# FFN entry in a two-layer decoder step: the chunk made beside the last tokens' sub-layer, in ordinary form

## Chip, cores and metric

The kernel runs on one NeuronCore of a Trainium2 chip. The metric is the time of one execution on the device in microseconds (us). Five engines work side by side, each on its own queue: TensorE (PE; its weight loads are PEld), VectorE (DVE), ScalarE (ACT), GpSimd (POOL) and SyncE (SP), which here issues most of the transfers. TensorE runs at one of two clock levels, 1.2 and 2.4 GHz; a granted clock of 1.00 is the upper one, 0.50 the lower.

## What is computed

One inference step over 1024 prompt tokens and 32 sample tokens, 1056 in all, model width 1024. Layer 0 mixes by pooling and a state-space recurrence, layer 1 by dilated attention; each ends in a SwiGLU feed-forward part (FFN) with 2816 hidden units. What matters here is the end of each mixing sub-layer and the start of its FFN:

```python
hp = hp + rms_norm(y_p, g[1])
hp = hp + rms_norm(swiglu_ffn(rms_norm(hp, g[2]), w_gate, w_up, w_down), g[3])
def swiglu_ffn(x, w_gate, w_up, w_down):
    return (jax.nn.silu(x @ w_gate) * (x @ w_up)) @ w_down
```

## The kernel before

**Numbers in two halves.** Every fp32 operand of a matmul is held as a rounded part `hi` and a rest `lo`, and a product is three matmuls (`mm3`, lines 171 to 173): hi by hi, lo by hi, hi by lo. A weight block is split by a cast on ACT (line 1140) and a subtraction on POOL or DVE (line 1141).

**Tokens.** The tokens are cut into four quarters: 0 and 2 of 256 columns, 1 and 3 of 272 (256 prompt tokens and 16 of the sample). Quarters 0 and 2 form pair 0, quarters 1 and 3 pair 1. Tile i is 128 tokens of a quarter; tile 8 is the 32 sample tokens.

**Seven products.** The FFN's first part multiplies a chunk of 256 hidden units (11 chunks, c = 0 to 10) by all tokens, once for the gate and once for up. It uses a scheme with seven products of 2 by 2 blocks in place of eight. Class `Blocks` keeps the blocks of the activations: B11 and B21 (the two halves of the features of the pair's first quarter), B22 (of the second) and the sums T1 to T4. Class `Weights` makes the sums S1 to S4 of the weights (four DVE additions, lines 1147, 1148, 1153, 1154, and the splits). `seven` runs the products; each is 12 matmuls for one pair, evacuated from PSUM by an addition on DVE (line 1172) or a copy on ACT (line 1174). `hidden` runs the gate and the up products of a chunk, applies silu (line 1195), multiplies the two (line 1199) and stores the result by a transfer from ACT's queue (line 1201).

**The boundary of a tile** (class `Boundary`, put in a pipeline by `Tiles`): `turn` transposes the projected tile on PE (line 318); `stats` takes its mean square (lines 207 to 211); `scale` and `residual` (lines 327 and 331) norm it and add the stream h; `stats2` and `scale2` (line 342) norm it for the FFN; `turn2` transposes it back (line 349); `first` splits it into blocks (lines 265 to 275), `second` (lines 279 to 281) and `third` (lines 286, 287) make T1 to T4 and split them. The transposes of all tiles share two PSUM buffers, `xs` and `tmp` have one buffer each, `h` two.

**The order.** `proj_out` projects quarters 0 and 2, then 1, then 3, each followed by the boundary of its tiles. Before the boundary of quarter 3 it yields to `ffn`, which first issues chunks 0 and 1 for pair 0, gate and up, in the projection's PSUM banks; then come the boundaries of tiles 6, 8 and 7, the last tokens. After them the PSUM banks are changed, and the FFN goes on with chunk 1 for pair 1 (its gate loaded a second time), chunk 0 for pair 1 (both weights loaded a second time), and chunks 2 to 10 for both pairs at once. The instructions are written in this order; a planner that simulates the engines then sets the order on each queue, by what its model finds ready.

Of the kernel before, what the change touches and what calls it, by code (L numbers as in the profile page):

```python
# [9 lines left out]
F32 = mybir.dt.float32  # L10
BF16 = mybir.dt.bfloat16
F32R = mybir.dt.float32r
AF = mybir.ActivationFunctionType
# [11 lines left out]
P = 128  # L25
# [12 lines left out]
HALF = NT // 2  # L38
HID = 2816
HT = HID // P  # L40
# [14 lines left out]
def dram_ap(base, offset, pattern):  # L55
    return bass.AP(tensor=base.tensor, offset=base.offset + offset, ap=[list(x) for x in pattern])
# [3 lines left out]
def step_kernel(ctx, tc, x_prompt, x_sample, state_pool, state_s5, cache_k, cache_v, norm_gains,  # L60
# [4 lines left out]
    nc = tc.nc  # L65
    taps = taps or {}
    V, A, G, T = nc.vector, nc.scalar, nc.gpsimd, nc.tensor
    mult, add, sub = ALU.mult, ALU.add, ALU.subtract
# [10 lines left out]
    wpool = ctx.enter_context(tc.tile_pool(name="wpool", bufs=3))  # L79
# [17 lines left out]
    def nm(s):  # L97
        uid[0] += 1
        return f"{s}_{uid[0]}"

    def mmbank():
        return banks[-1].pool.tile([P, 512], F32, name=nm("mm"), tag="mm", bufs=banks[-1].mm)
# [67 lines left out]
    def mm3(ps, wh, wl, xh, xl, start, stop):  # L170
        T.matmul(ps, wh, xh, start=start, stop=False)  # L171
        T.matmul(ps, wl, xh, start=False, stop=False)  # L172
        T.matmul(ps, wh, xl, start=False, stop=stop)  # L173
# [66 lines left out]
    class Blocks:  # L240
# [1 line left out]


        def __init__(self, xp, Y):
            self.xp, self.blk, self.made = xp, {}, {}
            self.homes = {0: (((Y.pool, "q0"), ("B11", "B21")), ((Y.pool, "q2"), ("T1", "T2")),
                              ((xp, "xc"), ("B22", "T3")), ((xp, "xd"), ("T4",))),
                          1: (((Y.pool, "q1"), ("B11", "B21")), ((Y.pool, "q3"), ("T1", "T2")),
                              ((xp, "xa"), ("T3",)), ((xp, "xb"), ("B22",)), ((xp, "xe"), ("T4",)))}
# [11 lines left out]
        def left(self, pair, c, pt):  # L261
            self.get("B11", pair)
            t = self.made[pair, ("B11", "B21")]
            hi, lo, src = t[:, :, 0, :, c], t[:, :, 1, :, c], pt.rearrange("p (a k) c -> p a k c", a=2)
            A.copy(hi, src)
            V.tensor_tensor(lo, src, hi.bitcast(F32), op=sub)

        def right1(self, part, pt, tmp):
            bc, t3, b11, b21 = tmp
# [19 lines left out]
        def first(self, i, pt, state):  # L289
            pair = 1 if i == 8 else i // 2 % 2  # L290
            c = slice(256, 272) if i == 8 else slice(i % 2 * P, i % 2 * P + P)
            if i < 4 or i == 8:
                self.left(pair, c, pt[:, :, 0:16] if i == 8 else pt)
            if i >= 4:
                state["part"] = lambda n, e: self.get(n, pair)[e][:, :, c]
                t = self.xp.tile([P, 4, 4, c.stop - c.start], F32, name=nm("tmp"), tag="tmp", bufs=1)
                state["tmp"] = [t[:, v] for v in range(4)]
                self.right1(state["part"], pt[:, :, 16:32] if i == 8 else pt, state["tmp"])

        def second(self, i, state):  # L300
            if state:
# [164 lines left out]
    for src in (lambda_re, lambda_im):  # L466
        raw = ptile("lamraw", P)
# [153 lines left out]
    for v, dst in enumerate((c1, c2)):  # L621
        pt = mmbank()
# [16 lines left out]
    for j in range(2):  # L639
# [6 lines left out]
        pt = mmbank()  # L646
# [470 lines left out]
    def ffn(layer, xS, Y, poc, after, side):  # L1117
# [6 lines left out]
        class Weights:  # L1124
# [6 lines left out]
            def split(self, early=False):  # L1131
                r0, r1 = (four(r) for r in self.raws)
                a11, a21, a12, a22 = r0[:, :, 0], r0[:, :, 1], r1[:, :, 0], r1[:, :, 1]
                new = lambda n: wpool.tile([P, 1024], F32R, name=nm(n), tag=n, bufs=4)

                def pair(src, two=True):
                    hi, lo = (new(n).rearrange("p (k i c) -> p k i c", k=4, i=2) for n in ("whi", "wlo"))
                    if not two:
                        hi, lo = hi[:, :, 0], lo[:, :, 0]
                    A.copy(hi, src)  # L1140
                    (V if early and src is S34 else G).tensor_tensor(lo, src, hi.bitcast(F32), op=sub)  # L1141
                    return hi, lo

                half = lambda t, i: (t[0][:, :, i], t[1][:, :, i])
                S12, S34 = (xS.pool.tile([P, 4, 2, P], F32, name=nm(n), tag=n, bufs=1) for n in ("S12", "S34"))
                self.w = {"A11": pair(a11, False)}
                V.tensor_tensor(S12[:, :, 0], a21, a22, op=add)
                V.tensor_tensor(S12[:, :, 1], S12[:, :, 0], a11, op=sub)
                t = pair(S12)
                self.w["S1"], self.w["S2"] = half(t, 0), half(t, 1)  # L1150
                t = pair(r1)
                self.w["A12"], self.w["A22"] = half(t, 0), half(t, 1)
                V.tensor_tensor(S34[:, :, 0], a11, a21, op=sub)
                V.tensor_tensor(S34[:, :, 1], a12, S12[:, :, 1], op=sub)
                t = pair(S34)
                self.w["S3"], self.w["S4"] = half(t, 0), half(t, 1)

        def seven(w, pairs, bank, C, evac):

            def prod(a, b):  # L1160
                ps = bank()
                o = 0
                for pair in pairs:
                    wh, wl = w.w[a]
                    bh, bl = blk[b, pair]
                    n = QUARTERS[pair][1]
                    for k in range(4):
                        mm3(ps[:, o:o + n], wh[:, k], wl[:, k], bh[:, k], bl[:, k], k == 0, k == 3)
                    o += n
                return ps  # L1170

            plus = lambda o, ps, x: V.tensor_tensor(o, ps, x, op=add)  # L1172
            c11, c22, c12, c21 = C
            A.copy(c11, prod("A11", "B11"))
            plus(c22, prod("S2", "T2"), c11)
            plus(c11, prod("A12", "B21"), c11)
            evac(c11, 0, 0)
            plus(c21, prod("S3", "T3"), c22)
            p5 = prod("S1", "T1")
            plus(c12, p5, c22)  # L1180
            plus(c22, p5, c21)
            evac(c22, 1, 1)
            plus(c12, prod("S4", "B22"), c12)
            evac(c12, 0, 1)
            plus(c21, prod("A22", "T4"), c21)
            evac(c21, 1, 0)

        def hidden(c, first, second, pairs, bank, tiles):

            t1, t2 = tiles(), tiles()  # L1190
            got = dict(zip(((0, 0), (1, 1), (0, 1), (1, 0)), t1))

            def act(w, o):
                if w.gate:
                    A.activation(o, o, AF.Silu)

            def put(o, i, j):
                act(second, o)
                (V if i == j == 0 or c < 2 else G).tensor_tensor(o, o, got[i, j], op=mult)
                o0 = j * HALF + (256 if pairs[0] else 0)  # L1200
                nc.scalar.dma_start(hd[2 * c + i][:, o0:o0 + o.shape[-1]], o)

            together = first.gate and pairs == (0,)
            seven(first, pairs, bank, t1, lambda o, i, j: None if together else act(first, o))
            if together:
                act(first, ct[:, 0:4])
            seven(second, pairs, bank, t2, put)

        def raws(kind):
            if kind:  # L1210
                t = xS.pool.tile([P, 2, 4, 256], F32, name=nm("raw2"), tag=kind, bufs=1)
                return [t[:, h] for h in range(2)]
            return [wraw().rearrange("p (k c) -> p k c", k=4) for _ in range(2)]
# [3 lines left out]
            x.split(c < 2 if w is w_gate else c == 1)  # L1217
            return x

        single = lambda: mmbank()[:, 0:256]  # L1220
        parts = lambda: iter([[ct[:, j] for j in range(4 * e, 4 * e + 4)] for e in range(2)]).__next__
        for c in range(2):
            wg, wu = split(w_gate, c, None), split(w_up, c, None if c else "xe")
            hidden(c, wg, wu, (0,), single, parts())
        for _ in poc:
            pass
        po.close()
# [2 lines left out]
        gb = Banks(nm("psumg"))  # L1230
        big = lambda: [f.pool.tile([P, HALF], F32, name=nm("c"), tag=f"c{j}", bufs=2) for j in range(4)]
        two = lambda: gb.pool.tile([P, 1024], F32, name=nm("pp"), tag="pp", bufs=4)[:, 256:256 + HALF]
        for c in (1, 0):
            if c == 0:
                wu = split(w_up, c, "tmp")
            hidden(c, wu, split(w_gate, c, None), (1,), lambda: two()[:, 256:HALF], lambda: [t[:, 256:HALF] for t in big()])
        for c in range(2, HT // 2):
            hidden(c, split(w_gate, c, None), split(w_up, c, "tmp"), (0, 1), two, big)
        gb.close()
        f.close()  # L1240
# [627 lines left out]
    class Chunk:  # L1868
# [12 lines left out]
        def parts(self):  # L1881
            if self.j0 + 1 < self.u.nb - 1:
                return ((slice(0, 2), slice(0, 256)),)
            return ((slice(0, 1), slice(0, 256)), (slice(1, 2), slice(P, 256)))
# [200 lines left out]
```

## Time and profile before

| | us |
|---|---|
| time, median of 3 runs (lowest to highest) | 2784.46 (2779.21 to 2788.11) |
| profiled execution: its own time | 2785.69 |
| its span, first to last instruction | 2783.9 |
| busy: PE / DVE / POOL / ACT | 2618.0 / 1701.7 / 1423.2 / 1122.9 |

Times in the rows are counted from the span's start. Durations of PE's matmuls overlap, since they are pipelined: the distance between two starts is what one costs. A duration on DVE or POOL holds the time for which the instruction was held up once it had begun.

### The profile page before, as it was taken

What the parts mean: (1) busy time and instruction counts of PE and PEld (TensorE: products, weight loads), DVE (VectorE), ACT (ScalarE), POOL (GpSimd) and SP (SyncE); (2) the same over time, 40 slices, a digit from 0 to 9 for tenths busy, and PEclk for the clock granted to TensorE, in tenths of its full rate; (3) what the DMA queues carried; (4) which work ended last, traced back from release to release, by engine and by line L of the source; (5) the groups of instructions that cost most, each with busy time, mean ns of one, the idle gap of its engine ahead of it and who ended that gap; (6) DMA issues with size and microseconds to landing.
All of it is one profiled execution on the core that took longest, in us unless ns stands there. A gap on an engine that the chain in (4) does not pass through costs nothing.

```text
span 2783.9 us, 49802 instructions
## 1 busy us (share of the span) xinstructions
PE 2618.0 (94%) x19508; PEld 2518.7 (90%) x19508; DVE 1701.7 (61%) x3119; ACT 1122.9 (40%) x2053; POOL 1423.2 (51%) x1016
## 2 busy tenths in 40 slices
PE   6779997999999999989999999998989999999998
PEld 6768997999999999989999777878979999999998
DVE  8757469755554355743443699993797555543555
ACT  4224465322222311333444688884653222233112
POOL 4964457554554544012554466665565555554440
PEclk9989998999999999999999999999989999999999
DMA  5254453322222422243887666664623222232223
GB/s 151 98 192 117 124 182 97 99 92 73 74 85 89 150 93 93 84 163 125 240 249 204 166 168 159 167 154 137 198 89 106 70 81 81 70 120 82 93 93 133
DMA packets 275662, 350.75 MB, mean 126 GB/s; under 512 B 44056, under 2 KB 208668, under 8 KB 275420
## 3 DMA queue, kind: packets, MB, share of 16 engines
q1 hardware_dynamic: 215252, 289.82, 35.4%
q10 hardware_dynamic: 59024, 53.55, 5.7%
q0 software_dynamic: 1152, 4.19, 0.4%
q8 instruction: 154, 2.52, 0.4%
q14 instruction: 80, 0.66, 0.1%
HBM read 268.29 MB, written 79.39 MB: 125 GB/s over the span
## 4 chain that ended last, share of the span: by engine, by line
PE 70%; DVE 12%; POOL 6%; DMA 4%; issue 4%; ACT 3%; SPq 1%; ACTq 0%; DVEq 0%; POOLq 0%
PE pp L172 9%; PE pp L171 9%; PE pp L173 9%; PE mm L171 7%; PE mm L172 6%; PE mm L173 6%; PE tp L172 2%; PE tp L171 2%; PE tp L173 2%; PE tq L171 2%; PE tq L172 2%; PE tq L173 2%; POOL e L529 2%; PE pt L1879 1%; POOL es L529 1%
## 5 line engine op out<-in xcount | busy, mean ns | idle before, releaser
L171 PE MATMUL pp<-blk,whi 128*128 128x272 f32 (+1 forms) x2240 | 638.8, 287 | 9.5 <-DVE ct L1172 9.3
L172 PE MATMUL pp<-blk,wlo 128*128 128x272 f32 (+1 forms) x2240 | 641.5, 288 | 1.9 <-DVE wlo L1141 1.9
L173 PE MATMUL pp<-blk,whi 128*128 128x272 f32 (+1 forms) x2240 | 638.8, 287 | 0.0
L142 POOL TENSOR_TENSOR wlo<-wraw,whi 128x1024 fp32r<-128x1024 f32 x102 | 246.1, 2422 | 558.0 <-ACT whi L141 534.2
L171 PEld LDWEIGHTS pp<-blk,whi 128*128 128x128 f32 x2240 | 426.2, 191 | 10.7 <-DVE ct L1172 9.7
L172 PEld LDWEIGHTS pp<-blk,wlo 128*128 128x128 f32 x2240 | 425.8, 191 | 2.3 <-DVE wlo L1141 2.3
L173 PEld LDWEIGHTS pp<-blk,whi 128*128 128x128 f32 x2240 | 425.8, 191 | 0.0
L1172 DVE TENSOR_TENSOR c<-pp,c 128x528 f32<-128x528 f32 (+1 forms) x308 | 202.0, 656 | 337.2 <-PE pp L173 329.8
L1141 POOL TENSOR_TENSOR wlo<-S,whi 128x1024 fp32r<-128x1024 f32 x90 | 220.1, 2445 | 360.2 <-ACT whi L1140 359.9
L141 ACT CAST whi<-wraw 128x1024 fp32r<-128x1024 f32 x126 | 131.1, 1053 | 363.8 <-PE mm L173 106.3
L1140 ACT CAST whi<-S 128x1024 fp32r<-128x1024 f32 x100 | 105.0, 1050 | 344.1 <-PE pp L173 314.9
L173 PE MATMUL mm<-hid,whi 128*128 128x256 f32 (+1 forms) x680 | 193.9, 286 | 8.1 <-POOL hid L1260 8.1
L171 PE MATMUL mm<-hid,whi 128*128 128x256 f32 (+1 forms) x680 | 197.3, 290 | 1.8 <-DVE yacc L1281 1.8
L172 PE MATMUL mm<-hid,wlo 128*128 128x256 f32 (+1 forms) x680 | 194.0, 285 | 0.0
L171 PE MATMUL mm<-y,whi 128*128 128x256 f32 (+1 forms) x576 | 166.6, 289 | 2.7 <-DVE s5o L1031 1.4
L173 PE MATMUL mm<-y,whi 128*128 128x256 f32 (+1 forms) x576 | 165.8, 288 | 0.0
L172 PE MATMUL mm<-y,wlo 128*128 128x256 f32 (+1 forms) x576 | 165.5, 287 | 0.0
L1281 DVE TENSOR_TENSOR yacc<-mm,yacc 128x272 f32<-128x272 f32 (+1 forms) x264 | 113.2, 431 | 81.4 <-PE mm L173 81.4
L171 PE MATMUL tp<-hid,whi 128*128 128x272 f32 x484 | 138.3, 286 | 0.0
L172 PE MATMUL tp<-hid,wlo 128*128 128x272 f32 x484 | 138.1, 285 | 0.0
L173 PE MATMUL tp<-hid,whi 128*128 128x272 f32 x484 | 137.6, 285 | 0.0
L1141 POOL TENSOR_TENSOR wlo<-wraw,whi 128x512 fp32r<-128x512 f32 (+1 forms) x56 | 117.8, 2103 | 36.0 <-ACT whi L1140 36.0
(521 smaller groups left out, 7662.4 us busy)
## 6 DMA issues: line engine op xcount, KB each, us to landing
wraw<-in_ffn_w_gate_dram SPq DMA_DIRECT2D x52, 512.0 KB
hid<-hd SPq DMA_DIRECT2D x44, 528.0 KB
raw<-in_ffn_w_up_dram SPq DMA_DIRECT2D x44, 512.0 KB
wraw<-in_ffn_w_down_dram SPq DMA_DIRECT2D x44, 512.0 KB
hd<-c ACTq DMA_DIRECT2D x72, 264.0 KB
wraw<-in_ab_w_out_dram SPq DMA_DIRECT2D x24, 512.0 KB
wraw<-in_c_w_qkv_dram ACTq DMA_DIRECT2D x24, 512.0 KB
kt<-in_cache_k_dram SPq DMA_DIRECT2D x32, 384.0 KB
```

What stands on the lines that cost most here:

```text
L141: A.copy(hi[:rows], raw[:rows])
L142: lo_eng.tensor_tensor(lo[:rows], raw[:rows], hi[:rows].bitcast(F32), op=sub)
L171: T.matmul(ps, wh, xh, start=start, stop=False)
L172: T.matmul(ps, wl, xh, start=False, stop=False)
L173: T.matmul(ps, wh, xl, start=False, stop=stop)
L529: eng.tensor_tensor(o, a, b, op=op)
L1140: A.copy(hi, src)
L1141: (V if early and src is S34 else G).tensor_tensor(lo, src, hi.bitcast(F32), op=sub)
L1172: plus = lambda o, ps, x: V.tensor_tensor(o, ps, x, op=add)
L1281: V.tensor_tensor(yo, ps[:, :n], yo, op=add)
L1879: T.transpose(pt[:, j, r * P:(r + 1) * P], self.u.rows[r].p[:, (self.j0 + j) * P:(self.j0 + j + 1) * P], ident)
```

## The change

Before the last tokens' boundary, only chunk 0 is made for pair 0, with the ordinary eight block products and no sums (`plain`): the gate's and the up weights are split as loaded, two blocks of 128 by 1024 each, and multiplied with B12 and B22, then with B11 and B21; all eight feature blocks accumulate in PSUM. B12 is therefore kept as well (`b12`: one cast and one subtraction for each of two tiles, in the places named S12 and S34 until the weights' sums need these). The gate's result leaves PSUM through silu on ACT, the up's through the multiplication on DVE (`put0`). After the last tokens' boundary chunk 0 follows for pair 1, with the gate first and the up weights loaded into the place `tmp`; chunk 1 is made for both pairs at once, like chunks 2 to 10.

```diff
+        def b12(self, c, pt):
+            if not self.extra:
+                self.extra = [self.xp.tile([P, 4, 256], F32R, name=nm("b12"), tag=t, bufs=1) for t in ("S12", "S34")]
+                self.blk["B12", 0] = tuple(self.extra)
+            hi, lo = (t[:, :, c] for t in self.extra)
+            A.copy(hi, pt[:, 0:4])
+            V.tensor_tensor(lo, pt[:, 0:4], hi.bitcast(F32), op=sub)
...
                 self.right1(state["part"], pt[:, :, 16:32] if i == 8 else pt, state["tmp"])
+                if pair == 0:
+                    self.b12(c, pt)
...
-            together = first.gate and pairs == (0,)
-            seven(first, pairs, bank, t1, lambda o, i, j: None if together else act(first, o))
-            if together:
-                act(first, ct[:, 0:4])
+            seven(first, pairs, bank, t1, lambda o, i, j: act(first, o))
...
-        for c in range(2):
-            wg, wu = split(w_gate, c, None), split(w_up, c, None if c else "xe")
-            hidden(c, wg, wu, (0,), single, parts())
+        def plain(w, kind, evac):
+            rs = raws(kind)
+            ws = []
+            for j, raw in enumerate(rs):
+                nc.sync.dma_start(raw, dram_ap(w, base + j * 512 * HID, [[HID, P], [P * HID, 4], [1, 256]]))
+                hi, lo = (wpool.tile([P, 1024], F32R, name=nm(n), tag=n, bufs=4).rearrange("p (k i c) -> p k i c", k=4, i=2)
+                          for n in ("whi", "wlo"))
+                A.copy(hi, four(raw))
+                G.tensor_tensor(lo, four(raw), hi.bitcast(F32), op=sub)
+                ws.append((hi, lo))
+            ps = [mmbank() for _ in range(2)]
+            for j, names in ((1, ("B12", "B22")), (0, ("B11", "B21"))):
+                for i in range(2):
+                    for half, name in enumerate(names):
+                        bh, bl = blk[name, 0]
+                        wh, wl = ws[half]
+                        for k in range(4):
+                            mm3(ps[i][:, j * 256:j * 256 + 256], wh[:, k, i], wl[:, k, i], bh[:, k], bl[:, k],
+                                half == 0 and k == 0, half == 1 and k == 3)
+            for i in range(2):
+                evac(i, ps[i], ct[:, 4 * (w is w_up) + 2 * i:4 * (w is w_up) + 2 * i + 2].rearrange("p a b -> p (a b)"))
+
+        def put0(i, ps, o):
+            V.tensor_tensor(o, ps, ct[:, 2 * i:2 * i + 2].rearrange("p a b -> p (a b)"), op=mult)
+            for j in range(2):
+                nc.scalar.dma_start(hd[i][:, j * HALF:j * HALF + 256], o[:, j * 256:j * 256 + 256])
+
+        plain(w_gate, None, lambda i, ps, o: A.activation(o, ps, AF.Silu))
+        plain(w_up, "xe", put0)
...
-        for c in (1, 0):
-            if c == 0:
-                wu = split(w_up, c, "tmp")
-            hidden(c, wu, split(w_gate, c, None), (1,), lambda: two()[:, 256:HALF], lambda: [t[:, 256:HALF] for t in big()])
-        for c in range(2, HT // 2):
+        hidden(0, split(w_gate, 0, None), split(w_up, 0, "tmp"), (1,), lambda: two()[:, 256:HALF],
+               lambda: [t[:, 256:HALF] for t in big()])
+        for c in range(1, HT // 2):
             hidden(c, split(w_gate, c, None), split(w_up, c, "tmp"), (0, 1), two, big)
```

## Rows read from the trace of the kernel before

**Rows 1.** The page: busy time, share of the span, instructions, by engine.
```profile
PE 2618.0 (94%) x19508; PEld 2518.7 (90%) x19508; DVE 1701.7 (61%) x3119; ACT 1122.9 (40%) x2053; POOL 1423.2 (51%) x1016
```
**Rows 2.** Windows: stretch, length, busy PE PEld DVE ACT POOL, granted clock, DMA share, GB/s.
```profile
416.00:491.20 75.20, 58.09 (x416) 54.96 (x415) 73.34 (x100) 40.04 (x67) 49.66 (x28) 0.87 0.29 92
2008.90:2084.40 75.50, 59.66 (x416) 56.64 (x416) 73.94 (x101) 40.03 (x67) 47.88 (x28) 0.85 0.29 91
470.00:480.00 10.00, 9.03 (x59) 8.74 (x60) 9.54 (x18) 4.28 (x10) 6.81 (x7) 0.75 0.19 52
534.05:575.40 41.35, 41.35 (x339) 41.35 (x337) 26.34 (x28) 11.51 (x16) 20.24 (x11) 1.00 0.23 69
```
**Rows 3.** Timeline of PE (start us, us; bracket: idle before, who ended it).
```profile
405.77 1.07 PE L318 MATMUL tp<-ident,yo 128*128 128x128 f32 x8 [1.44 <-DVE h L331]
416.02 0.28 PE L171 MATMUL mm<-blk,whi 128*128 128x256 f32 x1
426.26 1.03 PE L349 MATMUL tp<-ident,xs 128*128 128x128 f32 x8
431.65 1.04 PE L318 MATMUL tp<-ident,yo 128*128 128x128 f32 x8
474.12 1.54 PE L349 MATMUL tp<-ident,xs 128*128 128x128 f32 x8 [0.37 <-DVE xs L342]
488.06 0.60 PE L171 MATMUL pp<-blk,whi 128*128 128x272 f32 x1 [4.66 <-DVE ct L1172]
492.24 0.29 PE L172 MATMUL pp<-blk,wlo 128*128 128x272 f32 x1
534.05 0.28 PE L171 MATMUL pp<-blk,whi 128*128 128x256 f32 x1
```
**Rows 4.** Timeline of DVE, layer 0.
```profile
423.99 3.43 DVE L1141 TENSOR_TENSOR wlo<-S,whi 128x1024 fp32r<-128x1024 f32 x1
429.37 1.21 DVE L266 TENSOR_TENSOR blk<-tp,blk 128x1024 fp32r<-128x1024 f32 x1
490.47 0.68 DVE L287 TENSOR_TENSOR blk<-tmp,blk 128x512 fp32r<-128x512 f32 x1
```
**Rows 5.** Groups by line, DVE, 431.65 to 491.2 (count, busy us, mean ns, idle before).
```profile
L1172 DVE TENSOR_TENSOR ct<-mm,ct 128x256 f32<-128x256 f32 x27 | 10.4, 410 | 0.0
L1199 DVE TENSOR_TENSOR ct<-ct 128x256 f32<-128x256 f32 x8 | 7.7, 975 | 0.0
...
L1147 DVE TENSOR_TENSOR S<-wraw,wraw 128x512 f32<-128x512 f32 x3 | 3.2, 1069 | 0.0
L1148 DVE TENSOR_TENSOR S<-S,wraw 128x512 f32<-128x512 f32 x3 | 3.0, 1014 | 0.1
L1154 DVE TENSOR_TENSOR S<-wraw,S 128x512 f32<-128x512 f32 x3 | 2.8, 944 | 0.0
L1154 DVE TENSOR_TENSOR S<-raw,S 128x512 f32<-128x512 f32 x1 | 2.7, 2723 | 0.0
...
L1141 DVE TENSOR_TENSOR wlo<-S,whi 128x1024 fp32r<-128x1024 f32 x2 | 2.4, 1212 | 0.0
L1153 DVE TENSOR_TENSOR S<-wraw 128x512 f32<-128x512 f32 x3 | 2.0, 678 | 0.0
L1148 DVE TENSOR_TENSOR S<-S,raw 128x512 f32<-128x512 f32 x1 | 1.8, 1775 | 0.0
```
**Rows 6.** Groups by line, POOL, then ACT, 431.65 to 491.2.
```profile
L1141 POOL TENSOR_TENSOR wlo<-S,whi 128x1024 fp32r<-128x1024 f32 x4 | 10.7, 2672 | 6.9 <-ACT whi L1140 6.8
...
L1195 ACT ACT_TABLE_LOAD x2 | 2.6, 1283 | 0.0
```
**Rows 7.** Timelines of SP and POOL: up weights of chunk 0, second load.
```profile
491.22 0.96 SPq L1129 DMA_DIRECT2D raw<-in_ffn_w_up_dram  x2
508.24 2.58 POOL L1141 TENSOR_TENSOR wlo<-S,whi 128x1024 fp32r<-128x1024 f32 x1 [2.92 <-ACT whi L1140]
```
**Rows 8.** Window of tile raw: busy DVE ACT POOL, granted clock, DMA share, GB/s.
```profile
496.00:498.00 2.00, 0.00 (x0) 0.00 (x0) 0.00 (x0) 1.00 0.69 220
```

More of the change, by code (lines that the diff above doesn't have):

```diff
@@ L244, in __init__ @@
         def __init__(self, xp, Y):
-            self.xp, self.blk, self.made = xp, {}, {}
+            self.xp, self.blk, self.made, self.extra = xp, {}, {}, None
             self.homes = {0: (((Y.pool, "q0"), ("B11", "B21")), ((Y.pool, "q2"), ("T1", "T2")),
@@ L1218, in split @@
             return x
-        single = lambda: mmbank()[:, 0:256]
-        parts = lambda: iter([[ct[:, j] for j in range(4 * e, 4 * e + 4)] for e in range(2)]).__next__
-        for c in range(2):
-            wg, wu = split(w_gate, c, None), split(w_up, c, None if c else "xe")
-            hidden(c, wg, wu, (0,), single, parts())
+        def plain(w, kind, evac):
[25 more added lines that the diff above has]
+        plain(w_up, "xe", put0)
         for _ in poc:
```

## The prediction

> **What bounds the kernel now.** I read the page first: PE is busy 94% of the span [rows 1], so over most of it a change pays only if it takes matmuls away or lets them start earlier. Inside a chunk of the FFN that is so: the first chunk made for both pairs has PE busy for all of its 41.35 us, 336 matmuls at a granted clock of 1.00 [rows 2], 0.123 us each. Then I laid windows over the two FFN entries, from the first FFN matmul at 416.02 [rows 3] to the last instruction that makes a block of the last tokens, DVE's at 490.47 with 0.68, so at 491.15 [rows 4]. There the limit is another one: in 75.2 us DVE is busy for 73.34, PE for 58.09 at a granted clock of 0.87, and layer 1 shows the same stretch with 73.94 of 75.5 [rows 2]. The timelines say what DVE holds up. PE goes on with pair 1 at 488.06 and reaches chunk 2 at 534.05 [rows 3]; from there on both versions do the same, so I compare the time at which chunk 2 begins.
>
> The chain that sets the end of the stretch is that of the last tokens: the transposes of tile 6 start at 431.65 [rows 3], the last split of tile 7 ends at 491.15, 59.5 us later. Through it DVE also works for the FFN entry. Grouped by line from 431.65 on, the FFN's share is evacuations 10.4, multiplications 7.7, the weights' sums 3.2 + 3.0 + 2.8 + 2.7 + 2.0 + 1.8 and low halves 2.4 [rows 5]: 36.0 us of 59.5.
>
> **The change, part by part.** *Removed from the tail.* Of the five weights whose sums were made in the tail one stays, chunk 0's gate for pair 1. It keeps four additions at 0.678 and one low half at 1.212 [rows 5], 3.9 us. The plain chunk has two multiplications of 512 columns; no row shows them. Nearest are the 128x512 additions at 0.678 and the 256-column multiplications at 0.975 with what held them up, twice as wide 1.95 [rows 5]. I take 0.7, since one input comes from PSUM and the held-up time comes mostly from POOL work that shrinks; 1.4 us for two, at most 3.9. So 36.0 - 3.9 - 1.4 = 30.7 us of DVE work leave the 59.5. Ahead of it, tile 6 waited for a PSUM buffer freed by line 266, which started at 429.37, behind a low half at 423.99 of 3.43 and a sum [rows 4]. Without these it can start some 4.9 us earlier, and tile 6 at 426.8. If every removed microsecond was on the chain, it ends at 426.8 + 59.5 - 30.7 = 455.6.
>
> *Added to the tail.* The plain weights need four low halves on POOL, nearest row 2.67 each [rows 6], and silu is called twice on ACT, with a change of table of 1.283 [rows 6] there and back. One POOL subtraction (2.7) and one visit to silu (2 x 1.28 and about 1 for the work) ahead of the chain's own instructions give 6.2 us; none is the lower bound, all of them about 18 the upper. I take 6.2, because the low halves are due at the start, when tile 6 has just begun. The tail then ends at 461.8, 29.35 us earlier.
>
> *PE in the tail.* 192 matmuls replace 336, at 0.12 some 23 us. Behind 416.02, with the transposes, they are done around 450; the chain covers them. Were it shorter than 34 us they would set the end.
>
> *Moved behind the tail.* Before, 336 matmuls of pair 1 stand between 488.06 and 534.05: 45.99 us, 4.2 of them at the lower clock, until 492.24 [rows 3]. Afterwards there are 168 of pair 1, then the whole chunk 1. A matmul of 272 columns costs 0.123 x 272/264 = 0.127, so 84 cost 10.65. The gate costs 10.65 + 2.1 for the same slow start (half of 4.2) = 12.75, the up 10.65, chunk 1 costs 41.35.
>
> *The up weights of chunk 0* are loaded into `tmp`, which the last tokens' `third` frees. Before, SP issues that load at 491.22, with the end of the tail [rows 7]; its traffic ends within the window to 498 [rows 8], 6.8 after. One microsecond for cast and sums, then POOL: half a block 1.3 and three blocks at 2.67, so the fourth product's operand is there 17.1 after the tail. PE restarts 3.1 before the tail's end (488.06 against 491.15), and needs it 12.75 + 3 x 1.5 after that, at 14.25. A wait of 2.9, taken as 3. Before, another 21 us of pair-1 matmuls covered this load; that cover is gone. Together 12.75 + 3 + 10.65 + 41.35 = 67.75, against 45.99: 21.8 us more.
>
> *Ahead of the tail.* `b12` adds two DVE subtractions of 128x512 (0.678 each) and two casts per layer, while DVE feeds the projection; PE there waited 1.44 for DVE [rows 3]. I charge 1.4; nothing is the other bound.
>
> *At no cost:* the transfers. One load of 1 MB per layer falls away, four stores of 128 KB become part of wider ones, and the DMA share of the tail is 0.29 [rows 2]. The second gate load waits only for the plain gate's split, some 30 us before it is needed. Behind it on SP stand the tail's loads of h; they wait, as before, for the h buffers.
>
> **Sum.** Per layer 29.35 - 21.8 - 1.4 = 6.15 us, for two layers 12.3. The profiled span goes from 2783.9 to 2771.6 and that execution's own time from 2785.69 to about 2773.4; it stands 1.2 above the median of 2784.46, which goes to 2772.
>
> **One rule against it.** Transposes cost more where PE had paused: 1.03 at 426.26, 1.54 at 474.12 [rows 3], in a window of granted clock 0.75 [rows 2]. After the plain chunk PE has nothing but two such steps on the chain, 0.5 us each. The Trainium skill ("TensorE: Matmul & The Clock Gate", section "Why this matters for your kernels") advises against pauses between bursts of matmuls, as the clock then returns to its lower level; the trace agrees. By that rule the sum would come to 10.3 instead of 12.3, 2774.
>
> **The rivals.** (1) *The tail hardly shortens: slower.* DVE looks full because its two-input instructions are held up while POOL works: the sum S<-raw took 2.723 where the same shape took 0.678 [rows 5]. Then much of the removed work filled waits, and POOL's plain low halves (2.67 each) now stand before the tail's own POOL work. With a third of the 30.7 us on the chain the tail ends at 426.8 + 59.5 - 10.2 = 476.1. Per layer that is 15.05 - 21.8 - 1.4 = -8.15: 2801. It breaks even at 468.0 and is slower by 0.3% from 472.2 on. For it: POOL 49.66 us busy of 75.2 [rows 2]; against: POOL's FFN share falls too, from thirteen subtractions to about seven. The Trainium skill ("SBUF — State Buffer", section "Who interferes with whom") has one engine fully blocked while the other holds the pair of ports that they share; the trace agrees in the 2.723.
>
> (2) *The up weights come late: no change.* If the planner keeps the old order, the sums' low half ends on POOL at 508.24 + 2.58 [rows 7], 19.6 after the tail's end, and PE needs it at 11.15. The wait is 8.45 instead of 3: 0.7 us gained per layer, 2783.
>
> (3) *Everything goes well.* The tail ends at 455.6, with no wait for weights and `b12` hidden: 35.55 - 18.75 = 16.8 per layer, 2751.
>
> **Numbers.** A measurement of this kernel tells about 0.3%, 8.4 us, from no change. Forecast 0.50 (tail's end 458 to 466, times of 2764 to 2781); rival 1 0.20, rival 2 0.15, rival 3 0.15. Faster: 0.36 of the forecast and rival 3, 0.51. Same: 0.14 of the forecast, 0.05 of rival 1, 0.13 of rival 2, 0.32. Slower 0.17. The range takes in most of rivals 2 and 3 and half of 1: 2754 to 2794; the forecast's own is 2762 to 2782.
>
> **What would show it.** DVE clearly below full in the tail; last split of tile 7 near 462 (a sooner start of tile 6, near 427, first); PE idle or transposing from 450 until the restart near 459; a short wait of PE for a low half of the up weights 13 us after it; chunk 2 near 528 instead of 534, twice. Wrong if the tail ends after 468, if PE waits over 8 us for the up weights, or if the plain chunk starts late because its full blocks take longer to split than the half block before.

## The result, and the profile after

The changed kernel takes 2813.27 us (median of 4 runs, 2810.52 to 2819.3), the kernel before 2786.28 in the same session: a ratio of 1.0096, 95% interval 1.0081 to 1.0112. It is slower, and outside the predicted range. Lines of the listing have moved by 9 to 11 (L287 is now L296, L318 is L329, L342 is L353, L349 is L360, L1172 is L1183); L1252 is the plain chunk's multiplication, L1256 its silu. The experiments' listings have line numbers of their own; where a row below depends on one, the text names it.

The page's busy line, to be held against [rows 1]:

```profile
PE 2624.1 (93%) x19556; PEld 2527.7 (90%) x19556; DVE 1666.5 (59%) x3027; ACT 1112.8 (40%) x2033; POOL 1380.5 (49%) x1004
```

DVE has 35 us less to do, as the change meant, and PE 6 us more (48 more matmuls). The windows answer to [rows 2]: the entry of layer 0, two pieces of its end, chunk 1 for both pairs, and the entry of layer 1:

```profile
415.30:479.90 64.60, 40.61 (x281) 38.73 (x280) 41.11 (x49) 32.24 (x59) 29.90 (x21) 0.74 0.26 89
450.00:460.00 10.00, 3.88 (x16) 3.14 (x16) 9.07 (x12) 5.87 (x14) 0.00 (x0) 0.50 0.38 127
470.00:480.00 10.00, 4.76 (x21) 4.44 (x21) 6.86 (x10) 4.41 (x10) 7.04 (x7) 0.50 0.01 2
504.52:545.87 41.35, 41.35 (x338) 41.35 (x337) 26.57 (x30) 11.04 (x14) 12.76 (x6) 1.00 0.24 79
...
2028.00:2089.50 61.50, 38.31 (x280) 36.73 (x279) 39.67 (x48) 30.71 (x57) 29.94 (x21) 0.79 0.25 84
```

The entry is shorter, 64.6 us instead of 75.2, and DVE is no longer full in it. But PE idles 24.0 us there (64.6 - 40.6), where before it idled 17.1, and a whole chunk, 41.35 us, now stands behind it. Chunk 2 starts at 545.87 instead of 534.05, 11.8 later. PE's timeline shows why, against [rows 3]:

```profile
444.61 0.29 PE L173 MATMUL mm<-blk,whi 128*128 128x256 f32 x1
444.74 1.91 PE L329 MATMUL tp<-ident,yo 128*128 128x128 f32 x16
452.31 1.94 PE L329 MATMUL tp<-ident,yo 128*128 128x128 f32 x8 [5.66 <-DVE h L342]
456.14 1.94 PE L360 MATMUL tp<-ident,xs 128*128 128x128 f32 x8 [1.89 <-DVE rs L211]
...
467.56 1.94 PE L360 MATMUL tp<-ident,xs 128*128 128x128 f32 x8 [5.62 <-DVE xs L353]
...
477.46 0.60 PE L171 MATMUL pp<-blk,whi 128*128 128x272 f32 x1 [5.24 <-ACT blk L295]
477.85 0.43 PE L172 MATMUL pp<-blk,wlo 128*128 128x272 f32 x1
...
497.27 0.59 PE L171 MATMUL pp<-blk,whi 128*128 128x272 f32 x1 [2.73 <-DVE c L1183]
...
504.52 0.28 PE L171 MATMUL pp<-blk,whi 128*128 128x256 f32 x1
```

The transposes of tiles 6 and 8 (16 in one row, at 444.74) come directly behind the last plain matmul, with no idle time in front: at that moment they were not waiting for data but for their place in PE's queue. All 192 plain matmuls were put ahead of them (in the kernel before, 72 of the 336). DVE's timeline, against [rows 4], and one line of ACT's:

```profile
429.19 1.23 DVE L266 TENSOR_TENSOR blk<-tp,blk 128x1024 fp32r<-128x1024 f32 x1 [4.03 <-ACT blk L265]
437.62 0.69 DVE L1158 TENSOR_TENSOR S<-wraw,wraw 128x512 f32<-128x512 f32 x1 [7.20 <-PE mm L172]
...
478.35 1.46 DVE L296 TENSOR_TENSOR blk<-tmp,blk 128x512 fp32r<-128x512 f32 x2
...
491.24 2.87 DVE L1158 TENSOR_TENSOR S<-wraw,wraw 128x512 f32<-128x512 f32 x1 [1.39 <-POOL wlo L1152]
494.14 2.72 DVE L1159 TENSOR_TENSOR S<-S,wraw 128x512 f32<-128x512 f32 x1
496.79 0.97 DVE L1183 TENSOR_TENSOR c<-pp,c 128x272 f32<-128x272 f32 x2
```

```profile
428.14 1.01 ACT L265 CAST blk<-tp 128x1024 fp32r<-128x1024 f32 x1 [5.17 <-PE tp L360]
```

While the plain matmuls run, DVE idles for 7.20 us. The tail, from tile 6's transposes to the last split of tile 7, goes from 444.74 to 478.35 + 1.46 = 479.81, 35.1 us; before it took 59.5. Layer 1 shows the same: its first FFN matmul starts at 2027.98, and on PE and DVE stand

```profile
2054.45 1.91 PE L329 MATMUL tp<-ident,yo 128*128 128x128 f32 x16
```

```profile
2088.03 1.46 DVE L296 TENSOR_TENSOR blk<-tmp,blk 128x512 fp32r<-128x512 f32 x2
```

### The profile page after: what moved, and what is told of

It is laid out like the page before. It is cut to its first block, busy times and chain, and to the rows that moved or that the text cites. A ratio compares the mean times of both kernels' runs of the same rounds, so it can differ in the third digit from the quotient of the medians.

```text
span 2812.5 us, 49713 instructions
## 1 busy us (share of the span) xinstructions
PE 2624.1 (93%) x19556; PEld 2527.7 (90%) x19556; DVE 1666.5 (59%) x3027; ACT 1112.8 (40%) x2033; POOL 1380.5 (49%) x1004
## 4 chain that ended last, share of the span: by engine, by line
PE 74%; DVE 10%; DMA 5%; issue 4%; ACT 3%; POOL 2%; SPq 1%; ACTq 0%; POOLq 0%; DVEq 0%
PE pp L172 10%; PE pp L171 10%; PE pp L173 10%; PE mm L171 7%; PE mm L173 7%; PE mm L172 7%; PE tp L173 2%; PE tp L171 2%; PE tp L172 2%; PE tq L171 2%; PE tq L172 2%; PE tq L173 2%; PE pt L1910 1%; DVE pl L1927 1%; DVE Pr L1886 1%
## 5 line engine op out<-in xcount | busy, mean ns | idle before, releaser
L171 PE MATMUL pp<-blk,whi 128*128 128x272 f32 (+1 forms) x2352 | 673.6, 288 | 16.4 <-ACT blk L295 10.9
L172 PE MATMUL pp<-blk,wlo 128*128 128x272 f32 (+1 forms) x2352 | 676.3, 289 | 0.9 <-POOL wlo L1152 0.8
L173 PE MATMUL pp<-blk,whi 128*128 128x272 f32 (+1 forms) x2352 | 673.2, 287 | 0.0
L171 PEld LDWEIGHTS pp<-blk,whi 128*128 128x128 f32 x2352 | 450.2, 192 | 17.4 <-ACT blk L295 11.5
L172 PEld LDWEIGHTS pp<-blk,wlo 128*128 128x128 f32 x2352 | 449.8, 192 | 1.4 <-POOL wlo L1152 1.4
L173 PEld LDWEIGHTS pp<-blk,whi 128*128 128x128 f32 x2352 | 450.2, 192 | 0.0
L1183 DVE TENSOR_TENSOR c<-pp,c 128x528 f32<-128x528 f32 (+1 forms) x308 | 209.2, 680 | 357.1 <-PE pp L173 351.0
L1152 POOL TENSOR_TENSOR wlo<-S,whi 128x1024 fp32r<-128x1024 f32 x82 | 199.5, 2433 | 371.9 <-ACT whi L1151 371.7
L1151 ACT CAST whi<-S 128x1024 fp32r<-128x1024 f32 x88 | 92.4, 1050 | 356.4 <-PE pp L173 332.8
L173 PEld LDWEIGHTS mm<-hid,whi 128*128 128x128 f32 x680 | 128.7, 190 | 8.9 <-POOL hid L1291 8.9
```

## The experiments

Two theories. **A**: the change loses because its tail starts late (the transposes stand behind the plain matmuls in PE's queue) and because nothing of pair 0 is left for PE to do during it. **B**: the work that entry and tail share on DVE, POOL and ACT sets the end of the stretch, in whatever order; the loss is then chunk 1's new place behind the tail.

Layer 0, in us from the first FFN matmul; the tail goes from tile 6's transposes to the last split of tile 7. Where chunk 1 is made for both pairs at once, chunk 2 starts 41.35 behind it. The last column is the time from ACT's first copy of a projected block to chunk 2, both layers together, less that of the kernel before (438.6); each stems from one execution, and what the ratios say, times 2787, lies between 1.4 us below it and 5.3 above. The ratio is to runs of the kernel before beside it.

| kernel | median | ratio (95%) | tile 6 | tail's length, end | chunk 2 | stage |
|---|---|---|---|---|---|---|
| before | 2786 to 2788 | 1 | 15.6 | 59.5, 75.1 | 118.0 | 0 |
| after | 2813.3 | 1.0096 (1.0081 to 1.0112) | 29.5 | 35.1, 64.5 | 130.6 | +26.1 |
| E1 turns first | 2801.8 | 1.0047 (1.0030 to 1.0064) | 14.2 | 43.9, 58.1 | 124.4 | +14.5 |
| E2 tail first | 2805.6 | 1.0072 (1.0044 to 1.0099) | 12.8 | 46.5, 59.4 | 125.4 | +18.9 |
| E3 seven, second later | 2809.5 | 1.0080 (1.0053 to 1.0107) | 16.0 | 47.4, 63.4 | 129.3 | +20.9 |
| E4 after + chunk 1 | 2798.4 | 1.0038 (1.0023 to 1.0054) | 33.6 | 45.2, 78.9 | 120.6 | +6.4 |
| E5 E2 + chunk 1 | 2787.2 | 0.9991 (0.9977 to 1.0004) | 14.1 | 60.2, 74.4 | 114.9 | -2.4 |
| E6 before, tail first | 2790.4 | 1.0009 (0.9993 to 1.0024) | 15.2 | 63.6, 78.8 | 119.9 | +2.6 |
| E7 E2, silu late | 2807.0 | 1.0069 (1.0050 to 1.0088) | 11.5 | 42.1, 53.6 | 123.8 | +16.5 |
| E8 two plain, tail first | 2774.0 | 0.9954 (0.9939 to 0.9969) | 11.5 | 46.9, 58.4 | 108.2 | -18.1 |
| E9 two plain, turns first | 2806.6 | 1.0069 (1.0052 to 1.0086) | 13.1 | 69.6, 82.7 | 124.5 | +16.7 |

**E1: the turns of tiles 6 and 8 first.** `proj_out` hands over to the FFN only behind the first two tiles of quarter 3.

```diff
-            if q == 3:
-                yield po, ct
...
-            for t in todo:
+            for n, t in enumerate(todo):
+                if q == 3 and n == 2:
+                    yield po, ct
```

> The changed kernel, with the pipeline slots of tiles 6 and 8 issued ahead of the plain chunk, so that their 16 transposes stand in PE's order after 55 and 86 of its matmuls instead of after all 192; tile 7's stay behind all of them. Theory A (the tail starts late because its transposes stand behind the plain matmuls in PE's queue): tile 6 starts near 429 instead of 444.74, but tile 7's transposes still wait for the last plain matmul, near 447 instead of 452.31; the tail ends 5 to 7 us sooner than at 479.81, and the time falls by 10 to 14 us, to 2799 to 2803. Theory B (the tail's length is set by work that it shares with the FFN entry on DVE, POOL and ACT, and the loss is chunk 1's work placed behind it): tile 6 starts sooner, but the tail gets as much longer, and the time stays within 4 us of 2813.

PE's timeline of E1:

```profile
430.28 1.03 PE L329 MATMUL tp<-ident,yo 128*128 128x128 f32 x8
...
448.45 1.04 PE L329 MATMUL tp<-ident,yo 128*128 128x128 f32 x8
449.33 1.04 PE L360 MATMUL tp<-ident,xs 128*128 128x128 f32 x8
459.79 1.03 PE L360 MATMUL tp<-ident,xs 32*128 32x32 f32 x8 [9.42 <-DVE xs L353]
...
471.86 0.60 PE L171 MATMUL pp<-blk,whi 128*128 128x272 f32 x1 [4.30 <-ACT blk L295]
```

Tile 6 starts 15.3 us sooner by the stage's clock (14.2 instead of 29.5), and 0.0049 of the ratio's 0.0096 come back, 14 us of 27. The place in the queue was a cause, and the time is the one that A expected. But the tail grew from 35.1 to 43.9: tile 7's transposes, and the second ones of tile 6, still stand behind the plain matmuls, at 448.45 and 449.33.

**E2: the whole tail first.** The weights are split, then the whole boundary of tiles 6, 8 and 7 is issued, then the plain products.

```diff
-        def plain(w, kind, evac):
+        def plain_load(w, kind):
...
+            return ws
+
+        def plain(w, ws, evac):
...
+        pg, pu = plain_load(w_gate, None), plain_load(w_up, "xe")
         for _ in poc:
             pass
+        plain(w_gate, pg, lambda i, ps, o: A.activation(o, ps, AF.Silu))
+        plain(w_up, pu, put0)
```

> The changed kernel, with the loads and splits of the plain chunk's weights issued where they were, but its products issued after the whole tail, so that the planner fills the tail's gaps with them: in PE's order the transposes of tiles 6, 8 and 7 come after 55, 86 and 106 plain matmuls. Theory A: tile 6 starts near 429, tile 7 near 437, the tail takes its 35 us from tile 6 on and ends near 464; chunk 1 begins 15 us sooner than at 504.52, and the time falls by about 30 us, to 2778 to 2788, at or a little under the kernel before. Theory B: the tail, now beside the plain chunk's casts and subtractions, grows to 45 us or more; less than a third of that is gained, and the time stays above 2803.

No better than E1, though tile 7 no longer waits for the plain products; here B's expectation came true (a tail of 45 us or more, a time above 2803) and A's, 2778 to 2788, did not. ACT's timeline of E2 shows one candidate for a reason, changes of its table (L1263 is the plain gate's silu, L209 the root in the tail's statistics):

```profile
436.50 1.28 ACT L1263 ACT_TABLE_LOAD   x1
...
440.76 1.28 ACT L209 ACT_TABLE_LOAD   x1
...
443.40 1.28 ACT L1263 ACT_TABLE_LOAD   x1
...
445.31 1.28 ACT L209 ACT_TABLE_LOAD   x1
```

Four loads in 9 us stand in the tail's statistics (four in E1's tail as well, five in E8's, one in the changed kernel's). And PE runs out of work: at its restart it has idled for 8.11 us.

```profile
478.17 0.59 PE L171 MATMUL pp<-blk,whi 128*128 128x272 f32 x1 [8.11 <-ACT blk L295]
```

**E3: no plain form.** Chunk 0 by seven products as before, but alone in the entry, chunk 1 behind the tail for both pairs; `b12` is left out.

```diff
-        plain(w_gate, None, lambda i, ps, o: A.activation(o, ps, AF.Silu))
-        plain(w_up, "xe", put0)
+        single = lambda: mmbank()[:, 0:256]
+        parts = iter([[ct[:, j] for j in range(4 * e, 4 * e + 4)] for e in range(2)]).__next__
+        hidden(0, split(w_gate, 0, None), split(w_up, 0, "xe"), (0,), single, parts)
```

> Only the second half of the change: chunk 1 begins after the tail, but chunk 0 is made for pair 0 by seven products as before. PE's order around the tail's transposes is that of the kernel before. Theory A: the tail starts near 431.65 as before and loses only chunk 1's DVE work, some 18 us, of which a half to all counts: end between 473 and 482, chunk 2 between 538 and 547, and a time of 2794 to 2812, better than the changed kernel. Theory B: the loss is chunk 1's place alone, so that the time is that of the changed kernel, 2813, or more.

Here tile 6 starts at 16.0, as in the kernel before, and the ratio is 1.0080 all the same, not to be told from the changed kernel's 1.0096. So the later second chunk costs about as much as the whole change, without a plain product in sight. Between the theories the run does not decide: 2809.5 is at the upper end of A's range (2794 to 2812) and 3.5 us under B's.

**E4: the second chunk back in the entry.** The changed kernel, with chunk 1 for pair 0 by seven products behind the plain chunk, and pair 1 of chunks 1 and 0 behind the tail.

```diff
...
+        wg, wu = split(w_gate, 1, None), split(w_up, 1, None)
+        hidden(1, wg, wu, (0,), single, parts)
...
+        for c in (1, 0):
+            if c == 0:
+                wu = split(w_up, c, "tmp")
+            hidden(c, wu, split(w_gate, c, None), (1,), lambda: two()[:, 256:HALF], lambda: [t[:, 256:HALF] for t in big()])
```

> Only the first half of the change: chunk 0 for pair 0 in ordinary form, and chunk 1 for pair 0 in seven products beside the tail as before. In PE's order the transposes of tile 6 come only after 217 FFN matmuls (72 before). Theory A: tile 6 starts near 448, 16 us later than before, and with chunk 1's DVE work beside it the tail takes 40 to 45 us: end near 490, chunk 2 near 533 to 538, time 2784 to 2796, no better than before, although 12 us of DVE work are gone. Theory B: the work left out shows in full, the tail ends near 480, and the time is 2765 to 2772.

The tail starts even later (33.6), ends 14 us later than after, and still chunk 2 starts 10 us sooner: what PE does beside the tail is worth more here than the tail's end. The time, 2798.4, is near A's range (2784 to 2796) and far from B's (2765 to 2772), and inside neither.

**E5: both given back.** E2's order with E4's chunk 1, so behind E2's last line stands

```diff
+        single = lambda: mmbank()[:, 0:256]
+        parts = iter([[ct[:, j] for j in range(4 * e, 4 * e + 4)] for e in range(2)]).__next__
+        wg, wu = split(w_gate, 1, None), split(w_up, 1, None)
+        hidden(1, wg, wu, (0,), single, parts)
```

> Chunk 0's weights are split, then the whole boundary of tiles 6, 8 and 7 is issued, then chunk 0's plain products, and chunk 1 for pair 0 by seven products joins them in the entry, as cover; behind the boundary pair 1 of chunks 1 and 0 follows as in the kernel before. Theory A (the change loses because the tail starts behind 192 matmuls; give it PE's queue and leave enough pair-0 work behind it and the loss is gone): tile 6's transposes start 13 us after the first FFN matmul, the last split ends 62 to 68 us after it (75.1 before), chunk 2 starts at 107 to 113 us (118.0 before), so 5 to 11 us per layer less than before: 2765 to 2777. Theory B (the work that both share on DVE and POOL sets the end of the stretch, in whatever order): the tail grows by what is put beside it, ends at 75 us or later, and the time is that of the kernel before within 8 us, 2779 to 2795.

No difference from the kernel before that can be measured; the time is B's. Tile 6 starts where A has it, but the tail takes 60.2 us again. DVE's timeline of E5 shows how:

```profile
468.91 0.21 DVE L283 TENSOR_TENSOR tmp<-tp,tmp 128x64 f32<-128x64 f32 x1
...
474.28 2.08 DVE L296 TENSOR_TENSOR blk<-tmp,blk 128x64 fp32r<-128x64 f32 x1
...
477.42 0.21 DVE L296 TENSOR_TENSOR blk<-tmp,blk 128x64 fp32r<-128x64 f32 x1
...
478.88 0.69 DVE L283 TENSOR_TENSOR tmp<-tp,tmp 128x512 f32<-128x512 f32 x1 [0.31 <-issue]
```

The six small instructions of tile 8 stretch over 8.7 us, between evacuations (L1183) and sums of chunk 1, and tile 7, which needs the same buffer `tmp`, begins only behind them.

**E6: the order alone.** The kernel before with the tail issued ahead of both chunks' products.

```diff
+            if c == 0:
+                for _ in poc:
+                    pass
             hidden(c, wg, wu, (0,), single, parts())
-        for _ in poc:
-            pass
```

> The kernel before, with one thing changed: the whole boundary of tiles 6, 8 and 7 is issued ahead of the products of chunks 0 and 1 for pair 0 (the weights of chunk 0 are still split first). No plain product. Theory A (place in PE's queue): there PE has 72 matmuls ahead of tile 6, about 9 us, and the boundary waits for a PSUM buffer in any case, so the start of tile 6 hardly moves (15.6 us after the first FFN matmul) and the time stays within 4 us of before. Theory B (DVE sets the end): the same start, and the tail ends within 3 us of 75.1; the time again stays. If both are wrong and the order alone is worth time here too, tile 6 starts by 12 us, the tail ends by 68 and the time falls by 8 us or more. Slower by 8 us or more if the FFN's evacuations, now queued behind the boundary's work on DVE, let PE run dry before the restart.

No change that can be measured, as both theories had it: in the kernel before, tile 6 was not late in PE's queue, and starts at 15.2 instead of 15.6. The run tests the order only weakly, since some 60 of the FFN's matmuls still stand ahead of tile 6, where it was 72.

**E7: silu held back.** E2, with the plain gate's silu held until tile 7's T3 is split.

```diff
+        zero = xS.pool.tile([P, 1], F32, name=nm("zero"), tag="zero", bufs=1)
+        G.tensor_scalar(zero, blk["T3", 1][1][:, 0, 128:129].bitcast(F32), 0.0, None, op0=mult)
...
+            A.activation(late[i][1], late[i][0], AF.Silu, bias=zero)
```

> The order of the run with the whole boundary ahead of the plain products, and the plain gate's silu is held back until the last tokens' T3 is split (its bias is a zero made from that block), so that ACT changes its table only after the tail. Theory A' (two visits to silu, four table loads of 1.28 us, stand ahead of the statistics and splits of the last tokens and make their tail 11 us longer than in the changed kernel): the tail from tile 6's start to the last split falls from 46.5 to 36 to 41 us and the time from 2805.6 to 2786 to 2797. Rival (sums and low halves of chunk 0's second gate on DVE and POOL make it longer): the tail stays at 44 to 47 us and the time within 4 us of 2805.6.

A miss, with half a truth in it: the tail is 4.4 us shorter (42.1), but the time stays. PE's timeline of E7 shows where the gain went (L1256 is here the multiplication):

```profile
453.01 1.83 PE L360 MATMUL tp<-ident,xs 128*128 128x128 f32 x8 [2.49 <-DVE xs L353]
474.78 0.57 PE L171 MATMUL pp<-blk,whi 128*128 128x272 f32 x1 [19.95 <-DVE ct L1256]
```

PE goes on only when the late multiplication has emptied the projection's PSUM banks; it idles for 19.95 us.

**E8 and E9: both chunks in ordinary form.** `plain` for chunks 0 and 1; behind the tail, pair 1 of both. E8 issues the whole tail first (E2's order), E9 only the first half of tiles 6 and 8 (E1's).

```diff
...
+        for c in range(2):
+            pg, pu = plain_load(w_gate, c, None), plain_load(w_up, c, None if c else "xe")
+            if c == 0:
+                for _ in poc:
+                    pass
+            plain(w_gate, pg, lambda i, ps, o: A.activation(o, ps, AF.Silu))
+            plain(w_up, pu, lambda i, ps, o: put0(c, i, ps, o))
+        wu = split(w_up, 1, None)
...
```

> Both chunks 0 and 1 are made for pair 0 in ordinary form in the entry, with the whole boundary of tiles 6, 8 and 7 issued behind the splits of chunk 0's weights and ahead of all products; behind the boundary pair 1 of chunks 1 and 0 by seven products. Theory A (the change lost twice: the tail began behind the plain products, and chunk 1 for pair 0, which had covered PE during the tail, was moved behind it): with both given back, and without weights' sums on DVE, tile 6 starts 10 to 14 us after the first FFN matmul, the last split ends at 50 to 62, PE restarts by 64 and chunk 2 starts at 100 to 110 us (118.0 before): 8 to 16 us less per layer, 2757 to 2775. Theory B (work shared on POOL, ACT and DVE sets the end): eight plain low halves on POOL and four visits to silu on ACT make up for the sums, the tail ends at 68 to 78 us as in the run with chunk 1 by seven products, and the time is 2780 to 2795.

> As the run with both chunks in ordinary form, but only the first half of the boundary of tiles 6 and 8 is issued ahead of the entry, all else of the tail behind both chunks' products. Theory A: tiles 6 and 8 start at 10 to 14 us, tile 7 only behind most of the 384 plain matmuls, at 40 to 52, so the last split ends at 66 to 76 and chunk 2 starts at 110 to 118: 2772 to 2788, between the run with the whole tail first and the kernel before. Theory B (the shared work counts and not the place in PE's queue): the same time as the run with the whole tail first, within 4 us.

E8 beats both kernels (0.9954 of the kernel before, 0.9939 to 0.9969) at the upper end of what A gave (2774.0 of 2757 to 2775, chunk 2 at 108.2 of 100 to 110). Its entry up to the last split, PE's timeline (L1259 is here the multiplication) and DVE's last split:

```profile
415.40:473.90 58.50, 51.10 (x415) 50.03 (x414) 41.54 (x45) 37.45 (x64) 36.69 (x23) 0.97 0.35 117
```

```profile
426.95 1.03 PE L329 MATMUL tp<-ident,yo 128*128 128x128 f32 x8
...
479.22 0.36 PE L171 MATMUL pp<-blk,whi 128*128 128x272 f32 x1 [0.87 <-DVE ct L1259]
```

```profile
471.46 2.38 DVE L296 TENSOR_TENSOR blk<-tmp,blk 128x512 fp32r<-128x512 f32 x2
```

PE is busy for 51.1 of 58.5 us at a granted clock of 0.97. The tail is not short (46.9 us), but PE is still at plain products when it ends, and pair 1 starts 5 us behind its end. E9 does the same work in another order; its window and PE's timeline:

```profile
419.60:502.30 82.70, 61.52 (x473) 60.38 (x472) 46.00 (x55) 42.86 (x70) 39.64 (x26) 0.86 0.31 101
```

```profile
432.63 1.03 PE L329 MATMUL tp<-ident,yo 128*128 128x128 f32 x8
...
473.83 1.03 PE L329 MATMUL tp<-ident,yo 128*128 128x128 f32 x8
474.70 1.04 PE L360 MATMUL tp<-ident,xs 128*128 128x128 f32 x8
487.75 1.03 PE L360 MATMUL tp<-ident,xs 32*128 32x32 f32 x8 [12.01 <-DVE xs L353]
...
499.88 0.40 PE L171 MATMUL pp<-blk,whi 128*128 128x272 f32 x1 [3.66 <-ACT blk L295]
```

Tile 7's transposes, and the second transposes of tile 6, stand behind all plain products; then the rest of the tail runs with PE idle. The order alone is worth 2806.6 - 2774.0 = 32.6 us. A had expected E9 sooner (2772 to 2788, tile 7 by 52; it came at 54.2 and the tail ended at 82.7). B, which had E9 within 4 us of E8, is refuted as the rule; what stays of it is that a tail beside other work is longer. E5 and E8 issue the whole tail first and make both chunks in the entry; they differ in chunk 1's form for pair 0. By the ratios, 0.9991 and 0.9954, the ordinary form is then worth 10 us: the idea of the change pays where PE keeps its place and its work. Whether that comes from the sums taken off DVE or from matmuls that are ready sooner was not taken apart.

## Why the prediction was wrong

*DVE as the limit, and its relief: right.* Full before [rows 2], 41.1 of 64.6 us after.

*The step that failed: "tile 6 at 426.8".* It asked only when the PSUM buffer comes free on DVE, and not what stands ahead of the transposes in PE's queue. They started at 444.74, 17.9 later. Already the rows of before did not show the wait that the prediction read into them: the buffer was free at 429.37 + 1.21 = 430.58 [rows 4], and tile 6's transposes came at 431.65 with no idle time in front [rows 3], behind a matmul. The working had 192 plain matmuls "done around 450" with the chain beside them; they were put in front of it. Even the buffer came free no sooner, at 429.19 + 1.23 = 430.42 against 430.58: line 266 now waits 4.03 us for ACT, and ACT 5.17 for PE. None of the rivals named PE's queue; of the ways to be wrong, "the plain chunk starts late" was near and not it.

*The tail's length: right as a number, and largely by luck.* 35.0 was worked out, 35.1 measured. But this is the length of a tail that starts when the entry's work is over; the sums of chunk 0's second gate ran at 437.62, in DVE's wait. Where the tail started early without weights' sums for pair 0 beside it, it took 42.1 to 46.9 (E1, E2, E7, E8), and 69.6 in E9, where half of it stands behind all plain products. So 35.0 fails for the tail that the prediction described, which starts early beside the plain chunk, and an early start alone would not have saved the forecast: E1's tail ends at 474.2 and its time is 2801.8, which is rival 1 of the prediction (476.1 and 2801), and E2, where nothing of the tail stands behind the plain products, takes 2805.6. E7 puts up to 4.4 us of the growth down to silu's visits with their changes of ACT's table; the rest was not taken apart.

*Behind the tail: nearly right, in part by luck.* From the tail's end to chunk 2 the prediction had 534.05 - 491.15 + 21.8 = 64.7; measured 545.87 - 479.81 = 66.06. The wait of 3 us came (2.73), but for another reason: evacuations of pair 1 stood on DVE behind two weights' sums of 2.87 and 2.72 us, and no low half of the up weights was late.

*The sum.* In layer 1 tile 6 starts 26.5 us behind the first FFN matmul and the tail ends at 61.5, 35.0 again. The forecast had tile 6 at 426.8 - 416.02 = 10.8, so by this clock the failed step cost 29.5 - 10.8 = 18.7 in layer 0 and 15.7 in layer 1. Together they take 2772 to 2806; measured 2813.3. Of the rest, 3.8 us lie between chunk 2 of layer 0 and the first projected block of layer 1 (1376.3 against 1372.5; one execution each, and not explained). The added `b12` was not measured by itself: from the first projected block to the first FFN matmul the layers took 1.2 and 3.4 us longer than before, where 1.4 was charged.

*What the change did.* Given back to the changed kernel one at a time, the place in PE's queue is worth 14 us (E1; 7 in E2), the cover of the second chunk 16 (E4), both 29 (E5), and both with the second chunk in ordinary form too 40 (E8): the difference of the ratio from that of after, times 2787.

## What to carry to other kernels

When a chain's work is made lighter, look at each engine's queue for what will stand in front of the chain: matmuls that nothing interrupts are always ready, and a planner that goes by readiness puts them all first. Work that covers a latency-bound tail must be issued behind the tail's start and last to its end; moving it behind the tail to relieve one engine (DVE) leaves another (PE) idle. Price the tail's length for the place in which it will run, alone or beside other work.

## What the hardware showed beyond expectation

PE's clock met more of the tail than the two steps of 0.5 us that the prediction set aside. In the two windows of the tail the granted clock was 0.50, the lower level, with PE busy for 3.88 and 4.76 of 10 us; three groups of eight transposes took 1.94 us each instead of 1.03, 2.7 us more together, and matmuls of pair 1 0.43 instead of 0.29. The Trainium skill ("TensorE: Matmul & The Clock Gate", section "Why this matters for your kernels") warns of gaps between bursts; the trace agrees, and E8's entry, with few gaps, held 0.97.

ACT's table, changed back and forth between silu and the root, cost 1.28 us each time, four times in E2's tail. E8's tail has five, and E8 is the fastest run all the same.
